# 1 / rms as a power on GpSimd, the router's order written out, and the last tiles' buffers and squares

## The chip, the cores and the metric

The kernel runs on one core of a Trainium2 chip. Its engines each take their instructions in order: PE (TensorE, matrix products and transposes), DVE (VectorE), ACT (ScalarE), Pool (GpSimd) and SP (SyncE, which issues most DMAs). An engine waits on semaphores that the others raise. The metric is the device time of one execution in microseconds (us), here the median of three runs. The profile is of one more execution.

## The reference

Two blocks stand one behind the other, on 512 tokens of width 1024, and then 32 experts take two per token. Cut to what matters here:

```python
def rms_norm(x, g):
    xf = x.astype(jnp.float32)
    xf = xf * lax.rsqrt(jnp.mean(xf * xf, axis=-1, keepdims=True) + RMS_EPS)
    return xf.astype(x.dtype) * g

# first block: even mixer (window attention + retention), cross attention, odd mixer (convolution), cross attention
x = x + even_mixer(rmsnorm(x, e_norm[j]), ...)
x = x + memory_cross_attention(rmsnorm(x, c_norm[i]), rmsnorm(mem, c_mem_norm[i]), ...)
# retention ends each head with
o = o * lax.rsqrt(jnp.mean(o * o, axis=-1, keepdims=True) + EPS)
# second block: three branches, merged, then the router and the experts
x = x + merged @ w_out[l]
h2 = rms_norm(x, ffn_norm_g[l])
g_idx = jnp.argmax(h2 @ w_rg + b_rg); top_p, top_i = lax.top_k(softmax(e_logits of that group), 2)
y[e] = (silu(xb @ w_gate_e[e]) * (xb @ w_up_e[e])) @ w_down_e[e]      # for the tokens sent to expert e
x = x + sum over the token's two experts of weight * y
return rms_norm(x, final_norm_g)
```

## The kernel before

The 512 tokens are held feature-major: a tile of 128 features by 512 tokens for each of eight slices of the width. Almost all products up to 1318 us of the trace are made by `mm3` (L320, L321, L322), three fp32r matmuls for one product, and PE runs them back to back; weights come from HBM as `raw`, and ACT (L249) and DVE (L250) split them in a high and a low part.

**The norms.** For each of them a `Stats` object sums squares in `acc`. `total` (L281) adds them over partitions by four matmuls against ones, `mean` (L288) makes the mean on DVE, `norm_r` calls `rsqrt`, and the broadcast's PE transposes (L295, of a column `r_tok`, `rm_tok`, `n2r` or `rkv_tok`) spread the result over partitions. `rsqrt` (L229 to L244) is nine DVE instructions, most of them on 128x4: two integer steps for a first guess and seven arithmetic ones. It is called 14 times by the retention's four heads (L618), the norms and the router (L1248). Matmuls of other work stand on PE between L281 and L295. A tile scheduler fixes this order when the kernel is built; it is not decided at run time.

**The retention.** For a head, DVE sums squares (L615), makes the mean (L616), runs `rsqrt`, and multiplies the output `oc` by `rr` (L621); PE then transposes `oc` (L628). The state of a head is updated on DVE (L598, `st`), and PE multiplies with it (L607).

**The router.** `e_out(m)` (L1198 on) is called for the eight slices m of the merged output: xk (L1203, DVE), its square (L1205, ACT), four products with the router's weights (L1215, PE), for m = 7 the sums of squares (L1210, PE), four transposes (L1223), the token-major copy xt (L1226, ACT), for m = 7 the scaled copy xg (L1234, Pool) and its split in two parts h (L1236 on ACT, L1237 on Pool), and a store to `hd` in HBM (L1238, SP). Then v5 (L1247), `rsqrt`, the logits L (L1251), a chain of DVE instructions with the group's and the experts' maxima, PE's ranks (L1303), the slots (`slot_keys`, L1311 to L1314, with `key`; `slot_rows`, L1319 to L1331, with `pair`, `lane`, and for each k and t three or four rows `rv`), the count of rounds (`most`, `more`, `nri`), and `moe()`.

**The experts.** `moe()` runs 8 rounds of two pairs of experts. The first round's tokens are gathered by products with one-hot tiles `oh` (L1384, L1385, L1401); later ones by an indirect DMA (L1369) from `hd`. Weights, 96 MiB, come through a ring of 12 buffers `ew`, in 1 MiB transfers that SP issues (L1418, L1426); a transfer waits until PE has done with its buffer. `combine` adds the rounds by products with `comb` (L1483) and adds to `xts` on DVE (L1485, the tile's name in the trace is `merged`).

**The end.** `finish(t)` (L1488) runs for the four tiles of 128 tokens: Pool multiplies the first half with the gain (L1493, `zf`), ACT squares the tile and sums (L1494), DVE makes 1 / rms in seven steps (L1495 to L1504) and the second half of y (L1506), ACT the first half (L1508), and SP stores both (L1507, L1509). The four `zf` come from three buffers.

Of the kernel before, what the change touches and what calls it, by code (L numbers as in the profile page):

```python
# [20 lines left out]
D = 1024  # L21
# [2 lines left out]
EPS = 1e-6  # L24
NE, NL = 4, 8
HEAD0 = 2
FETCH = range(1, 8)
NEG = -1e30


# [133 lines left out]
def body(ctx: ExitStack, tc, A, out):  # L164
# [60 lines left out]
    def V(name, k, n=1):  # L225
        o, _ = VOFF[name]
        return vec[:, o + k:o + k + n]

    def rsqrt(dst, v, n):  # L229

        y = small(n, "rs_y")
        t = small(n, "rs_t", I32)
        b = small(n, "rs_b")
        nc.vector.tensor_scalar(t, v.bitcast(I32), 1, None, op0=ALU.arith_shift_right)
        nc.vector.tensor_scalar(y.bitcast(I32), t, -1, 0x5f3759df, op0=ALU.mult, op1=ALU.add)

        nc.vector.tensor_tensor(b, y, y, op=ALU.mult)
        nc.vector.tensor_tensor(b, v, b, op=ALU.mult)
        nc.vector.scalar_tensor_tensor(b, b, -10.0 / 3, b, op0=ALU.add, op1=ALU.mult)
        nc.vector.scalar_tensor_tensor(y, b, 5.0, y, op0=ALU.add, op1=ALU.mult)  # L240
        c = 0.375
        nc.vector.tensor_tensor(b, y, y, op=ALU.mult)
        nc.vector.scalar_tensor_tensor(b, v, -0.5 * c ** 3, b, op0=ALU.mult, op1=ALU.mult)
        nc.vector.scalar_tensor_tensor(dst, b, 1.5 * c, y, op0=ALU.add, op1=ALU.mult)  # L244

    def split(hi, lo, src, scale=None):

# [951 lines left out]
    def e_out(m, ps):  # L1199
        xk = r_xk()  # L1200
        nc.gpsimd.dma_start(xk, xd[m])
        nc.gpsimd.tensor_tensor(xk, xk, rb1, op=ALU.mult)
        nc.vector.scalar_tensor_tensor(xk, xk, V("final_norm", m), ps, op0=ALU.mult, op1=ALU.add)  # L1203
        sq = acc5 if m == 0 else r_gg()
        nc.scalar.activation(sq, xk, AF.Square)  # L1205
        if 0 < m < 7:
            nc.gpsimd.tensor_tensor(acc5, acc5, sq, op=ALU.add)
        def squares(a, last):
            for t in range(4):
                nc.tensor.matmul(lp[:, 144 + t:145 + t], lhsT=a[:, t * 128:t * 128 + 128], rhs=ones,  # L1210
                                 start=False, stop=last and t == 3)

        for t in range(4):
            c = slice(t * 128, t * 128 + 128)
            nc.tensor.matmul(lg[:, t], lhsT=xk[:, c], rhs=rtw[:, m], start=m == 0 and t == 0, stop=False)  # L1215
        if m == 7:
            squares(sq, True)
        if m == 6:
            squares(acc5, False)
# [97 lines left out]
    def slot_rows(ps):  # L1317

        TT(rtmp2, one2, pair0[:, None, None, :].to_broadcast([128, 2, 4, 32]), op=ALU.mult)  # L1319
        vsum(pair2, rtmp2)  # L1320
        STT(lane2, pair2, -128.0, key2, op0=ALU.mult, op1=ALU.add)
        for k in range(2):
            for t in range(4):
                lh = rp.tile([128, 128], F32, name="lh", tag="lh", bufs=2)
                rv = rp.tile([128, 3, 16], F32, name="rv", bufs=2)
                TS(lh, iota[:, :128], lane[k][:, t:t + 1], None, op0=ALU.is_equal)
                TS(rv[:, 1], iota[:, :16], pair[k][:, t:t + 1], 0.5, op0=ALU.is_equal, op1=ALU.mult)
                TS(rv[:, 0], rv[:, 1], tok[:, t:t + 1], 2.0, op0=ALU.mult, op1=ALU.mult)
                TS(rv[:, 2], rv[:, 1], (w1, w2)[k][:, t:t + 1], 2.0, op0=ALU.mult, op1=ALU.mult)
                TS(rv[:, 1], rv[:, 1], r5[:, t:t + 1], None, op0=ALU.mult)  # L1330
                nc.tensor.matmul(ps, lhsT=lh, rhs=rv.rearrange("p a b -> p (a b)"), start=k == 0 and t == 0,  # L1331
                                 stop=k == 1 and t == 3)
                yield k, t
        nc.vector.tensor_copy(rh, ps[:, 16:32])
        STT(rr, rh, 2.0, rh, op0=ALU.mult, op1=ALU.mult)
        nc.vector.tensor_copy(wt, ps[:, 32:48])
        TS(st, ps[:, :16], -1.0, None, op0=ALU.add)
        TS(st2, st, 0.0, None, op0=ALU.max)
        nc.vector.tensor_copy(sti, st2)
        TS(st2, st, -256.0, None, op0=ALU.add)  # L1340

    slot_keys(pre)
    nc.vector.tensor_copy(rank, pre)

    pn = trps()[:, :32]
    for t in range(4):
# [24 lines left out]

    def gather(j2, between=lambda: None):

        oh, kk, xT = [], [], []
        if j2 not in FETCH:
            for k in range(2):
                x_ = key[k]
                if j2:
                    x_ = hp.tile([128, 4], F32, name="kk", tag="kk", bufs=4)
                    TS(x_, key[k], -256.0 * j2, None, op0=ALU.add)  # L1380
                kk.append(x_)
            for t in range(4):
                x_ = hp.tile([128, 256], F32R, name="oh", tag="oh", bufs=5)
                TS(x_, iota, kk[0][:, t:t + 1], None, op0=ALU.is_equal)  # L1384
                STT(x_, iota, kk[1][:, t:t + 1], x_.bitcast(F32), op0=ALU.is_equal, op1=ALU.add)  # L1385
                oh.append(x_)
        for f2_ in range(4):
            if f2_ % 2 == 0:
                xs = xy.tile([128, D], F32, name="xT", tag="xT", bufs=3).rearrange("p (a i s) -> p a i s", a=2, i=2)
            ps = pq.tile([128, 2, 256], F32, name="pg", tag="pg", bufs=2)  # L1390
            for i in range(2):
                f = 2 * f2_ + i
                if j2 in FETCH:
                    for k in range(2):
                        nc.tensor.transpose(ps[:, i, k * 128:k * 128 + 128], fetched[j2][k][:, f * 128:f * 128 + 128],  # L1395
                                            ident)
                    continue
                for t in range(4):
                    c = slice(t * 128, t * 128 + 128)
                    for part in range(2):  # L1400
                        nc.tensor.matmul(ps[:, i], lhsT=h2[f][part][:, c], rhs=oh[t],  # L1401
                                         start=t == 0 and part == 0, stop=t == 3 and part == 1)
            between()
            x_ = xs[:, f2_ % 2]
# [83 lines left out]
    def finish(t, fg, y):  # L1488

        H = D // 2  # L1490
        ss = small(1, "fss")
        zf = xy.tile([128, D], F32, name="zf", tag="xT", bufs=3)
        nc.gpsimd.tensor_tensor(zf[:, :H], xts[t][:, :H], fg[:, :H], op=ALU.mult)  # L1493
        nc.scalar.activation(y, xts[t], AF.Square, accum_out=ss)  # L1494
        TS(ss, ss, 0.5 / D, 0.5 * EPS, op0=ALU.mult, op1=ALU.add)  # L1495
        rf, b, i = small(1, "frr"), small(1, "rs_b"), small(1, "rs_t", I32)
        TS(i, ss.bitcast(I32), 1, None, op0=ALU.arith_shift_right)  # L1497
        TS(rf.bitcast(I32), i, -1, 0x5f3759df - (1 << 22) - (1 << 31), op0=ALU.mult, op1=ALU.add)

        STT(b, rf, ss, rf, op0=ALU.mult, op1=ALU.mult)  # L1500
        STT(b, b, -5.0 / 3, b, op0=ALU.add, op1=ALU.mult)  # L1501
        STT(rf, b, 1.25, rf, op0=ALU.add, op1=ALU.mult)  # L1502
        STT(b, rf, ss, rf, op0=ALU.mult, op1=ALU.mult)  # L1503
        STT(rf, b, -2.0 / 3, rf, op0=ALU.add, op1=ALU.mult)  # L1504
# [6 lines left out]
    def moe():  # L1511
# [11 lines left out]
        last = []  # L1523
        for i in range(8):
            a, b, more_ = 2 * i, 2 * i + 1, i < 7
            if i + 1 in FETCH:
                fetched[i + 1] = fetch(i + 1)
            pa = gu(a, xT, wga)
            if more_:
# [26 lines left out]
        nc.vector.tensor_scalar(fg, fg, 3.375, None, op0=ALU.mult)  # L1556
        for t in combine(last):
            finish(t, fg, ew()[:, :D])

# [35 lines left out]
```

## Time and profile before

| | us |
|---|---|
| median of 3 runs (range) | 1618.24 (1617.14 to 1618.45) |
| the profiled execution | 1614.45 |
| its span, first to last instruction | 1612.7 |
| PE busy | 1557.1 (97%) |
| DVE busy | 915.5 (57%) |
| ACT busy | 604.8 (38%) |
| Pool busy | 115.5 (7%) |
| PE waiting for another engine or a DMA, all together | 36.8 |

The span is what the page of the profile covers; about 1.75 us of the execution lie around it. The mean granted TensorE clock is 0.991 of full speed. The page cuts the span in 40 slices of 40.3 us; slices 33 to 39 are the router, the experts and the end.

### The profile page before, as it was taken

The numbers are of one execution on the slowest core, as the hardware profiler recorded it, in microseconds if no ns is written. First come the engines' busy times: TensorE is split into PE (matmuls) and PEld (weight loads), VectorE is DVE, ScalarE is ACT, GpSimd is POOL, SyncE is SP. The second block draws the span as 40 slices with busy tenths as digits, with TensorE's granted clock in tenths as the row PEclk, the third lists the DMA queues.
The fourth block names the chain that finished last, engine by engine and source line by source line (L and its number), as shares of the span: only waits on it lengthen the run. The fifth ranks groups of instructions, "written<-read, shape, count | busy, mean of one in ns | idle before, by whom it ended". The sixth has DMA issues, their size and how long they took to land. (4 is left out here: it accounts for less than half of the span.)

```text
span 1612.7 us, 20331 instructions
## 1 busy us (share of the span) xinstructions
PE 1557.1 (97%) x7958; PEld 1206.7 (75%) x7958; DVE 915.5 (57%) x1697; ACT 604.8 (38%) x1060; POOL 115.5 (7%) x104
## 2 busy tenths in 40 slices
PE   7999999999999999999999999999999978999996
PEld 6758898888888889888887777888888865454443
DVE  5577675456555565555776776485544555343335
ACT  5455244344323244434545554244433421111212
POOL 0000200000011110000100000000111340000001
PEclk9999999999999999999999999999999989999998
DMA  6312244221222235320411112333422439999993
GB/s 213 105 53 79 79 134 154 82 76 53 105 81 103 104 131 183 105 105 26 165 54 55 54 55 80 110 137 114 165 105 93 142 93 369 419 421 420 420 420 138
DMA packets 44375, 241.91 MB, mean 150 GB/s; under 512 B 6112, under 2 KB 11104, under 8 KB 18160
## 3 DMA queue, kind: packets, MB, share of 16 engines
q1 hardware_dynamic: 40944, 228.93, 37.9%
q0 software_dynamic: 3328, 11.60, 2.0%
q8 instruction: 65, 1.06, 0.3%
q14 instruction: 38, 0.31, 0.1%
HBM read 234.22 MB, written 6.29 MB: 149 GB/s over the span
## 5 line engine op out<-in xcount | busy, mean ns | idle before, releaser
L249 ACT ACTIVATE w<-raw 128x1024 fp32r<-128x1024 f32 (+2 forms) x242 | 234.1, 968 | 413.7 <-PE mm L322 377.4
L320 PE MATMUL mm<-xg,w 128*128 128x512 f32 x864 | 341.3, 395 | 8.6 <-ACT xg L252 7.9
L321 PE MATMUL mm<-xg,w 128*128 128x512 f32 x864 | 341.3, 395 | 0.0
L322 PE MATMUL mm<-xg,w 128*128 128x512 f32 x864 | 340.3, 394 | 0.8 <-DVE w L250 0.8
L250 DVE TENSOR_TENSOR w<-raw,w 128x1024 fp32r<-128x1024 f32 (+2 forms) x242 | 280.0, 1159 | 105.6 <-ACT w L249 104.3
L320 PEld LDWEIGHTS mm<-xg,w 128*128 128x128 f32 x864 | 163.4, 189 | 42.2 <-ACT xg L252 7.9
L322 PEld LDWEIGHTS mm<-xg,w 128*128 128x128 f32 x864 | 163.1, 189 | 34.4 <-DVE w L250 1.2
L321 PEld LDWEIGHTS mm<-xg,w 128*128 128x128 f32 x864 | 163.1, 189 | 34.1 <-issue 2.0
L321 PE MATMUL mm<-y,w 128*128 128x512 f32 x448 | 174.9, 390 | 0.0
L322 PE MATMUL mm<-y,w 128*128 128x512 f32 x448 | 174.9, 391 | 0.0
L320 PE MATMUL mm<-y,w 128*128 128x512 f32 x448 | 174.3, 391 | 0.0
L1436 PE MATMUL pgu<-ew,xT 128*64 128x512 f32 x512 | 112.8, 594 | 0.0
L320 PEld LDWEIGHTS mm<-y,w 128*128 128x128 f32 x448 | 83.9, 188 | 17.7 <-ACT y L249 1.2
L321 PEld LDWEIGHTS mm<-y,w 128*128 128x128 f32 x448 | 84.2, 188 | 17.2 <-DVE y L250 0.4
L322 PEld LDWEIGHTS mm<-y,w 128*128 128x128 f32 x448 | 84.2, 188 | 17.2
L1436 PEld LDWEIGHTS pgu<-ew,xT 128*64 128x64 f32 x512 | 36.1, 137 | 71.0 <-issue 71.0
L1483 PE MATMUL py<-ys,comb 128*128 128x512 f32 x256 | 62.3, 397 | 0.0
L1443 DVE SCALAR_TENSOR_TENSOR eth<-eth,pgu 128x256 f32<-128x256 f32 x16 | 6.7, 422 | 95.1 <-ACT eth L1442 95.1
L1462 PE MATMUL py<-ew,aT 128*64 128x512 f32 x256 | 58.1, 596 | 1.2 <-ACT aT L1452 1.2
L1483 PEld LDWEIGHTS py<-ys,comb 128*128 128x128 f32 x256 | 46.9, 188 | 15.9 <-issue 5.7
L1442 ACT ACTIVATE eth<-pgu,rh 128x256 f32<-128x256 f32 x16 | 7.6, 474 | 130.8 <-PE pgu L1436 130.8
L389 DVE TENSOR_TENSOR x<-mm,x 128x512 f32<-128x512 f32 x32 | 22.1, 692 | 50.1 <-PE mm L322 50.1
(446 smaller groups left out, 2475.9 us busy)
## 6 DMA issues: line engine op xcount, KB each, us to landing
ew<-in_egu_dram SPq DMA_DIRECT2D x64, 1024.0 KB, 17.5
ew<-in_edn_dram SPq DMA_DIRECT2D x32, 1024.0 KB, 18.5
raw<-in_wkv_dram SPq DMA_DIRECT2D x20, 1024.0 KB, 4.7
raw<-in_ow_dram SPq DMA_DIRECT2D x16, 1024.0 KB, 4.7
raw<-in_ew_dram SPq DMA_DIRECT2D x12, 1024.0 KB, 4.8
raw<-in_w2gate_dram SPq DMA_DIRECT2D x12, 1024.0 KB, 4.8
raw<-in_wq_dram SPq DMA_DIRECT2D x8, 1024.0 KB, 4.8
raw<-in_wo_dram SPq DMA_DIRECT2D x8, 1024.0 KB, 4.7
```

The lines of the kernel that those rows point to most:

```text
L249: nc.scalar.activation(hi, src, AF.Copy)
L250: nc.vector.tensor_tensor(lo, src, hi.bitcast(F32), op=ALU.subtract)
L320: nc.tensor.matmul(ps, lhsT=lh, rhs=rh, start=first, stop=False)
L321: nc.tensor.matmul(ps, lhsT=lh, rhs=rl, start=False, stop=False)
L322: nc.tensor.matmul(ps, lhsT=ll, rhs=rh, start=False, stop=last)
L389: nc.vector.tensor_tensor(x[:, m], ps, x[:, m], op=ALU.add)
L1436: nc.tensor.matmul(ps[64 * i:64 * i + 64], lhsT=xT[k][:, o + 64 * i:o + 64 * i + 64], rhs=W[2 * (k // 4) + i][:, k % 4], start=k == 0, sto ...
L1442: nc.scalar.activation(th, pg_[:, :256], AF.Tanh, scale=rh[:, j:j + 1])
L1443: STT(th, th, 1.0, pg_[:, :256], op0=ALU.add, op1=ALU.mult)
L1462: nc.tensor.matmul(py[64 * i:64 * i + 64], lhsT=aT[:, f, 64 * i:64 * i + 64], rhs=W[i][:, f, n * 512:n * 512 + 512], start=f == 0, stop=f ...
L1483: nc.tensor.matmul(py, lhsT=comb[:, t * 128:t * 128 + 128], rhs=y[:, c], start=i == 0, stop=i == len(parts) - 1)
```

## The change

Three parts. First, `rsqrt` becomes one Pool instruction, v to the power of -0.5, against a constant tile `nhalf` (128x8); `finish` calls it too, with the gain scaled by 32 and the sum of squares plus D * EPS. Second, the router: for m = 7, xk and its square are made in two halves of 256 columns, and the transposes, xt, xg, h and the store of m = 7 (now `flipped(7)`) stand behind the power on Pool, in an order written out; `slot_rows` makes each `rv` by three instructions that don't hang on each other, with r5h = 0.5 * r5; the one-hots are four tiles of their own (`oh0`), made on DVE right behind `slot_keys`, in an order written out, ahead of the copy `rank`. Third, the end: tile 3's `zf` has a buffer of its own, and its squares are made in two halves.

```diff
+    nhalf = cp.tile([128, 8], F32, name="nhalf")
+    nc.vector.memset(nhalf, -0.5)
+
     def rsqrt(dst, v, n):
 
-        y = small(n, "rs_y")
-        t = small(n, "rs_t", I32)
-        b = small(n, "rs_b")
...
-        nc.vector.scalar_tensor_tensor(dst, b, 1.5 * c, y, op0=ALU.add, op1=ALU.mult)
+        nc.gpsimd.tensor_tensor(dst, v, nhalf[:, :n], op=ALU.pow)
...
-        nc.vector.scalar_tensor_tensor(xk, xk, V("final_norm", m), ps, op0=ALU.mult, op1=ALU.add)
         sq = acc5 if m == 0 else r_gg()
-        nc.scalar.activation(sq, xk, AF.Square)
+        for h in range(1 if m < 7 else 2):
+            c = slice(0, 512) if m < 7 else slice(h * 256, h * 256 + 256)
+            nc.vector.scalar_tensor_tensor(xk[:, c], xk[:, c], V("final_norm", m), ps[:, c], op0=ALU.mult, op1=ALU.add)
+            nc.scalar.activation(sq[:, c], xk[:, c], AF.Square)
...
     rsqrt(r5, v5, 4)
+
+    r5h = rtile("r5h", 4)
+    with tc.manual_schedule(engines={mybir.EngineType.Pool}):
+        nc.gpsimd.tensor_scalar(r5h, r5, 0.5, None, op0=ALU.mult)
+        flipped(7, late[0])
...
-                TS(rv[:, 1], iota[:, :16], pair[k][:, t:t + 1], 0.5, op0=ALU.is_equal, op1=ALU.mult)
-                TS(rv[:, 0], rv[:, 1], tok[:, t:t + 1], 2.0, op0=ALU.mult, op1=ALU.mult)
-                TS(rv[:, 2], rv[:, 1], (w1, w2)[k][:, t:t + 1], 2.0, op0=ALU.mult, op1=ALU.mult)
-                TS(rv[:, 1], rv[:, 1], r5[:, t:t + 1], None, op0=ALU.mult)
+                for a, v in enumerate((tok, r5h, (w1, w2)[k])):
+                    TS(rv[:, a], iota[:, :16], pair[k][:, t:t + 1], v[:, t:t + 1], op0=ALU.is_equal, op1=ALU.mult)
...
-    slot_keys(pre)
-    nc.vector.tensor_copy(rank, pre)
+    with tc.manual_schedule(engines={mybir.EngineType.DVE}):
+        slot_keys(pre)
+        one_hots()
+        nc.vector.tensor_copy(rank, pre)
...
-        zf = xy.tile([128, D], F32, name="zf", tag="xT", bufs=3)
+        zf = xy.tile([128, D], F32, name="zf", tag="xT" if t < 3 else "xg", bufs=3 if t < 3 else 2)
...
+        if t < 3:
+            nc.scalar.activation(y, xts[t], AF.Square, accum_out=ss[:, :1])
+            TS(ss[:, :1], ss[:, :1], D * EPS, None, op0=ALU.add)
+        else:
+            for h in range(2):
+                c = slice(h * H, h * H + H)
+                nc.scalar.activation(y[:, c], xts[t][:, c], AF.Square, accum_out=ss[:, h:h + 1])
+            STT(ss[:, :1], ss[:, :1], D * EPS, ss[:, 1:], op0=ALU.add, op1=ALU.add)
+        rsqrt(rf, ss[:, :1], 1)
```

With the nine instructions gone the scheduler also orders anew. On PE at the kernel's first norm, before (L320 to L322 are the products of the even mixer's input):

```order
L281 MATMUL tr<-ones,acc 128x1 x4
L320 MATMUL mm<-xg,w 128x512
L321 MATMUL mm<-xg,w 128x512
L322 MATMUL mm<-xg,w 128x512
...
L321 MATMUL mm<-xg,w 128x512
L322 MATMUL mm<-xg,w 128x512
L295 MATMUL tr<-ident,r_tok 128x128 x4
```

and now (the lines of the file have moved by 11, so L309 to L311 are the products, L284 the transposes):

```order
L270 MATMUL tr<-ones,acc 128x1 x4
L309 MATMUL mm<-xg,w 128x512
L310 MATMUL mm<-xg,w 128x512
L284 MATMUL tr<-ident,r_tok 128x128 x4
L311 MATMUL mm<-xg,w 128x512
```

Nine matmuls stood between the sums and the transposes that need r, and now two. It is the same at the other norms: 13 and now 2 at the odd mixer's, 16 and now 2 at `rkv_tok`, 9 and now 3 at `n2r`, 16 and now 1 at the first `rm_tok`, 12 and now 6 at the second.

On DVE in the retention, at the second head's sums, before (`st` is the state that PE's L607 waits for):

```order
L616 TENSOR_SCALAR ss<-ss 128x4
L234 TENSOR_SCALAR rs_t<-ss 128x4
...
L239 SCALAR_TENSOR_TENSOR rs_b<-rs_b 128x4
L598 SCALAR_TENSOR_TENSOR st<-st,sc 128x128
L240 SCALAR_TENSOR_TENSOR rs_y<-rs_b,rs_y 128x4
L598 SCALAR_TENSOR_TENSOR st<-st,sc 128x128
...
L244 SCALAR_TENSOR_TENSOR rr<-rs_b,rs_y 128x4
L621 TENSOR_SCALAR oc<-oc,rr 128x128 x4
```

and now:

```order
L605 TENSOR_SCALAR ss<-ss 128x4
L610 TENSOR_SCALAR oc<-oc,rr 128x128 x4
L587 SCALAR_TENSOR_TENSOR st<-st,sc 128x128 x2
L599 SCALAR_TENSOR_TENSOR oc<-tr,qdec,oc 128x384
L619 SCALAR_TENSOR_TENSOR gate<-tr,gate 128x512
```

The state's update stood inside the chain of nine, and now stands behind `oc`, which waits for Pool's `rr`. Two of the four heads have this form.

On Pool, at the end of the router (L1234 and L1237 are xg and h of m = 7 and keep their numbers; `misc` is the sum of squares of the slices before) and at the end of the kernel, now:

```order
L1198 TENSOR_TENSOR misc<-misc,gg 128x512
L233 TENSOR_TENSOR r_10586<-v_10585,nhalf 128x4
L1252 TENSOR_SCALAR r5h<-r_10586 128x4
L1234 TENSOR_TENSOR xg<-merged,gb 128x512
L1237 TENSOR_TENSOR h_10599<-xg,h_10599 128x512
...
L1494 TENSOR_TENSOR zf<-merged,ew 128x512 x2
L233 TENSOR_TENSOR frr<-fss,nhalf 128x1
L1494 TENSOR_TENSOR zf<-merged,ew 128x512
L233 TENSOR_TENSOR frr<-fss,nhalf 128x1
L1494 TENSOR_TENSOR zf<-merged,ew 128x512
L233 TENSOR_TENSOR frr<-fss,nhalf 128x1 x2
```

Before, xg and h followed `misc` at once, and the four `zf` stood in a row with nothing between. On DVE at the end, each tile's second half of y now stands ahead of the next tile's sum, and on ACT the first two tiles' y ahead of the third tile's squares, where before all four squares stood ahead of the four y.

## Rows read from the trace of the kernel before

**Rows 1.** The head of the page: the span, and the busy time of the engines with its share and the instructions.

```profile
span 1612.7 us, 20331 instructions
...
PE 1557.1 (97%) x7958; PEld 1206.7 (75%) x7958; DVE 915.5 (57%) x1697; ACT 604.8 (38%) x1060; POOL 115.5 (7%) x104
```

**Rows 2.** The waits of PE over the whole span, by the line that waits and by what ended the wait: total us, times, longest.

```profile
PE tr L1303 <- DVE hot L1299: 8.7, 1, 8.7
...
PE pg L1401 <- DVE oh L1385: 3.0, 1, 3.0
PE po L1215 <- DVE xk L1203: 2.6, 2, 1.3
...
PE tr L628 <- DVE oc L621: 1.4, 1, 1.4
...
PE tr L295 <- DVE rm_tok L244: 0.4, 1, 0.4
...
PE tr L295 <- DVE n2r L244: 0.2, 1, 0.2
```

**Rows 3.** The timeline at the first norm, 24 to 36 us: start, duration, engine and line; in brackets the idle time before and what ended it.

```profile
24.89 0.16 DVE L288 TENSOR_SCALAR mean<-tr 128x4 f32<-128x4 f32 x1 [1.23 <-PE tr L281]
...
25.27 0.40 PE L322 MATMUL mm<-xg,w 128*128 128x512 f32 x1
...
26.68 0.16 DVE L244 SCALAR_TENSOR_TENSOR r_tok<-rs_b,rs_y 128x4 f32<-128x4 f32 x1
...
26.89 0.65 PE L295 MATMUL tr<-ident,r_tok 128*128 128x128 f32 x4
```

**Rows 4.** Groups of instructions of Pool, different shapes apart: count, busy us in all, mean ns of one, idle before.

```profile
L1493 POOL TENSOR_TENSOR zf<-merged,ew 128x512 f32<-128x512 f32 x4 | 5.2, 1301 | 69.1 <-DVE merged L1485 65.1 <-ACT ew L1508 3.5 <-DVE frr L1498 0.5
...
L1079 POOL MEMSET pu<- 128x48 f32 x4 | 0.5, 137 | 88.7 <-DVE pool L1091 58.5 <-PE po L322 30.2
...
L1583 POOL MEMSET const-float32-1.0<- 128x1 f32 x1 | 0.1, 102 | 0.0
```

**Rows 5.** The timeline of the retention's second head, 151 to 161 us.

```profile
155.91 0.17 DVE L616 TENSOR_SCALAR ss<-ss 128x4 f32<-128x4 f32 x1
...
157.05 0.29 DVE L598 SCALAR_TENSOR_TENSOR st<-st,sc 128x128 f32<-128x128 f32 x1
...
157.43 0.83 PE L607 MATMUL tr<-st,rot 128*128 128x128 f32 x6
...
158.16 0.88 DVE L621 TENSOR_SCALAR oc<-oc,rr 128x128 f32<-128x128 f32 x4
```

**Rows 6.** The timeline of the router, 1311 to 1362 us.

```profile
1319.29 0.63 ACT L1205 ACTIVATE gg<-xk 128x512 f32<-128x512 f32 x1 [5.03 <-DVE xk L1203]
...
1321.88 0.16 DVE L1247 TENSOR_SCALAR v<-po 128x4 f32<-128x4 f32 x1 [2.63 <-PE po L1210]
...
1322.87 1.26 POOL L1234 TENSOR_TENSOR xg<-merged,gb 128x512 f32<-128x512 f32 x1 [10.16 <-DVE rs_b L238]
1322.88 1.27 DVE L239 SCALAR_TENSOR_TENSOR rs_b<-rs_b 128x4 f32<-128x4 f32 x1
1324.16 0.63 ACT L1236 ACTIVATE h<-xg 128x512 fp32r<-128x512 f32 x1 [1.37 <-POOL xg L1234]
...
1324.87 1.26 POOL L1237 TENSOR_TENSOR h<-xg,h 128x512 fp32r<-128x512 f32 x1 [0.74 <-ACT h L1236]
1324.96 0.74 DVE L1251 SCALAR_TENSOR_TENSOR L<-po,r,bb 128x36 f32<-128x36 f32 x4
...
1326.83 0.28 DVE L1280 TENSOR_TENSOR lane_e<-L,go 128x128 f32<-128x128 f32 x1
...
1331.73 0.28 DVE L1343 COPY rank<-tr 128x128 f32<-128x128 f32 x1
...
1335.08 0.88 DVE L1385 SCALAR_TENSOR_TENSOR oh<-iota,key,oh 128x256 fp32r<-128x256 bf16 x2
1335.87 0.42 DVE L1319 TENSOR_TENSOR rtmp<-one,c_pair 128x256 f32<-128x256 f32 x1
```

**Rows 7.** The timeline near the end, 1588 to 1613 us.

```profile
1594.15 1.30 POOL L1493 TENSOR_TENSOR zf<-merged,ew 128x512 f32<-128x512 f32 x1 [0.29 <-DVE merged L1485]
...
1594.83 0.14 DVE L1495 TENSOR_SCALAR fss<-fss 128x1 f32<-128x1 f32 x1
...
1595.13 0.69 DVE L1485 TENSOR_TENSOR merged<-py,merged 128x512 f32<-128x512 f32 x1
...
1595.96 1.34 POOL L1493 TENSOR_TENSOR zf<-merged,ew 128x512 f32<-128x512 f32 x1 [0.51 <-DVE frr L1498]
...
1596.65 0.67 DVE L1501 SCALAR_TENSOR_TENSOR rs_b<-rs_b 128x1 f32<-128x1 f32 x1
...
1598.94 1.06 ACT L1494 ACTIVATE ew<-merged 128x1024 f32<-128x1024 f32 x1 [1.02 <-DVE merged L1485]
...
1604.37 0.72 ACT L1508 ACTIVATE ew<-zf,frr 128x512 f32<-128x512 f32 x1 [0.61 <-DVE frr L1504]
```

**Rows 8.** The timeline, SP's issue of the last two expert weights (1 MiB each) and PE's first matmuls with the last of them.

```profile
1560.51 0.84 SPq L1426 DMA_DIRECT2D ew<-in_edn_dram  x2
...
1586.62 3.65 PE L1462 MATMUL py<-ew,aT 128*64 128x512 f32 x16 [0.72 <-ACT aT L1452]
```

**Rows 9.** The DMA issues of 1559 to 1563 us: count, KB each, median us from issue to landing.

```profile
ew<-in_edn_dram SPq DMA_DIRECT2D x2, 1024.0 KB, 18.7
```

More of the change, by code (lines that the diff above doesn't have):

```diff
@@ L26 @@
 HEAD0 = 2
-FETCH = range(1, 8)
 NEG = -1e30
@@ L227, in V @@
         return vec[:, o + k:o + k + n]
+    nhalf = cp.tile([128, 8], F32, name="nhalf")
+    nc.vector.memset(nhalf, -0.5)
     def rsqrt(dst, v, n):
-        y = small(n, "rs_y")
-        t = small(n, "rs_t", I32)
-        b = small(n, "rs_b")
[L234 to L243, printed above, removed]
-        nc.vector.scalar_tensor_tensor(dst, b, 1.5 * c, y, op0=ALU.add, op1=ALU.mult)
+        nc.gpsimd.tensor_tensor(dst, v, nhalf[:, :n], op=ALU.pow)
     def split(hi, lo, src, scale=None):
@@ L1217, in e_out, with flipped @@
             squares(sq, True)
-        if m == 6:
-            squares(acc5, False)
+            late.append(xk)
+        else:
+            if m == 6:
+                squares(acc5, False)
+            flipped(m, xk)
+    late = []
+    def flipped(m, xk):
         pt = trps()
@@ L1340, in slot_rows, with one_hots @@
         TS(st2, st, -256.0, None, op0=ALU.add)
-    slot_keys(pre)
-    nc.vector.tensor_copy(rank, pre)
+    oh0 = [rtile(f"oh{t}", 256, dt=F32R) for t in range(4)]
+    def one_hots():
+        for t, o in enumerate(oh0):
+            TS(o, iota, key[0][:, t:t + 1], None, op0=ALU.is_equal)
+            STT(o, iota, key[1][:, t:t + 1], o.bitcast(F32), op0=ALU.is_equal, op1=ALU.add)
+    with tc.manual_schedule(engines={mybir.EngineType.DVE}):
+        slot_keys(pre)
+        one_hots()
+        nc.vector.tensor_copy(rank, pre)
     pn = trps()[:, :32]
@@ L1372, in gather @@
     def gather(j2, between=lambda: None):
[L1374 to L1386, printed above, removed]
+        xT = []
         for f2_ in range(4):
@@ L1392, in gather @@
                 f = 2 * f2_ + i
-                if j2 in FETCH:
+                if j2:
                     for k in range(2):
@@ L1400, in gather @@
                     for part in range(2):
-                        nc.tensor.matmul(ps[:, i], lhsT=h2[f][part][:, c], rhs=oh[t],
+                        nc.tensor.matmul(ps[:, i], lhsT=h2[f][part][:, c], rhs=oh0[t],
                                          start=t == 0 and part == 0, stop=t == 3 and part == 1)
@@ L1490, in finish @@
         H = D // 2
-        ss = small(1, "fss")
-        zf = xy.tile([128, D], F32, name="zf", tag="xT", bufs=3)
+        ss, rf = small(2, "fss"), small(1, "frr")
+        zf = xy.tile([128, D], F32, name="zf", tag="xT" if t < 3 else "xg", bufs=3 if t < 3 else 2)
         nc.gpsimd.tensor_tensor(zf[:, :H], xts[t][:, :H], fg[:, :H], op=ALU.mult)
[L1494 to L1504, printed above, removed]
+        if t < 3:
+            nc.scalar.activation(y, xts[t], AF.Square, accum_out=ss[:, :1])
+            TS(ss[:, :1], ss[:, :1], D * EPS, None, op0=ALU.add)
+        else:
+            for h in range(2):
[3 more added lines that the diff above has]
+        rsqrt(rf, ss[:, :1], 1)
         o = out[0, t * 128:t * 128 + 128]
@@ L1525, in moe @@
             a, b, more_ = 2 * i, 2 * i + 1, i < 7
-            if i + 1 in FETCH:
+            if more_:
                 fetched[i + 1] = fetch(i + 1)
@@ L1555, in moe @@
         nc.sync.dma_start(fg, A["fing"].to_broadcast([128, D]))
-        nc.vector.tensor_scalar(fg, fg, 3.375, None, op0=ALU.mult)
+        nc.vector.tensor_scalar(fg, fg, 32.0, None, op0=ALU.mult)
         for t in combine(last):
@@ L1569, in body @@
         slot_keys(rtmp)
+        one_hots()
         with tc.manual_schedule(engines={mybir.EngineType.PE}):
```

## The prediction

> **What bounds the kernel now.** First the head of the page [rows 1]: PE is busy for 1557.1 of 1612.7 us, no other engine for more than 57%. So an edit counts only where PE waits for it, or where PE has nothing left to do. Next the waits of PE [rows 2], which add to 36.8 us. The reader is to see that the greatest, 8.7 us, is the router's chain on DVE (PE's ranks wait for `hot`), with 3.0 us for the first one-hots and 2.6 us for the last xk; the retention's `oc` costs 1.4 us once, and the norms' columns only 0.4 and 0.2 us. Then the timelines of the first norm [rows 3], the retention [rows 5], the router [rows 6] and the end [rows 7], for who follows whom. Last, whether the experts' weights would swallow what the router gains [rows 8, 9]: the last two transfers are issued at 1560.51 and land 18.7 us later, so at 1579.2 or, counted from the issue's end, 1580.1; PE first uses them at 1586.62. That leaves some 6.5 us of slack, and PE is the bound of the rounds. A round's transfers wait for PE to free buffers, so an earlier start of PE starts them earlier too. A microsecond gained ahead of the experts therefore reaches the end.
>
> **The unknown price d.** Everything hangs on how long one power takes on Pool; no row shows one. Pool's nearest rows [rows 4]: a memset of 128x1 takes 0.10 us and one of 128x48 0.14 us, which bounds d from below; a product of 128x512 takes 1.30 us, which bounds it from above for 1 to 8 columns, unless the power costs more than some hundred times a product for each element. That a power beats 0.10 us is excluded by the memset, which computes nothing. The shape (128x4, 128x1) is near the memsets, the function dearer than a product. I take d = 0.3 us, an estimate near the low end, and keep 0.10 and 1.26 for the range. A handover between engines is about 0.1 us each way: xg ends on Pool at 1324.13 and ACT begins at 1324.16; h ends on ACT at 1324.79 and Pool begins at 1324.87 [rows 6].
>
> **Part 1: the norms.** The nine instructions took from 24.89 + 0.16 to 26.68 + 0.16, so 1.8 us [rows 3], and nine matmuls lay beside them: PE waited for nothing there. Now two lie there. The mean ends at 25.05; the power runs from about 25.15 to 25.15 + d; PE has done with its two matmuls when the third of before begins, 25.27 [rows 3]. The transposes can go at about 25.25 + d, so PE idles for about d. Five norms have one to three matmuls of cover and cost d each (the one with six has more than they need and is counted at nothing). What goes is the wait of before, 0.4 + 0.2 us [rows 2]; `n2r` keeps its 0.2, since its transposes stood late already with nine matmuls of cover. Term: **0.4 - 5d**. The matmuls that stood there stand behind now, the same ones: no work is saved or added on PE.
>
> **Part 2: the retention.** The wait of 1.4 us for `oc` [rows 2] goes: with one instruction in place of nine, `oc` is early. But two heads have `st` behind `oc`. Before, the second head's mean ended at 156.08 and `st`'s first update at 157.34, and PE began with it at 157.43 [rows 5]. Now: power from 156.2 to 156.2 + d, `oc` takes 0.88, `st` 0.29, so `st` at 157.45 + d: 0.1 + d later, twice, and PE is waiting there. Term: 1.4 - 2(0.1 + d) = **1.2 - 2d**.
>
> **Part 3: the router.** From the mean (1321.88) to `lane_e` (1326.83) are 4.95 us before [rows 6]. In place of the nine: the mean 0.16, two handovers 0.2, d, the logits 0.74, and from their end (1325.70) to `lane_e` 1.13 as before, together 2.23 + d. Against that, two products of Pool, xg and h, move from beside `rsqrt` to beside the chain of maxima. One such meeting is in the trace: while Pool's xg runs (1322.87, 1.26 us), the DVE instruction that begins at 1322.88 takes 1.27 us, the mean beside it in the chain 0.16 [rows 6]; the logits, which read PSUM, run at 1324.96 beside Pool's h and aren't held. Now xg begins right behind r5h, beside the logits, and holds the first of the maxima's two-input steps for about 0.46 us; the Exp stands behind the copy h on ACT (0.38); h's 1.26 us hold a third step for 0.94. Sum 1.8, so 4.05 + d, and the chain gains 0.9 - d.
>
> The Trainium skill, SBUF — State Buffer, section "Who interferes with whom", speaks against this part of the change: VectorE and GpSimd share one port pair under an exclusive lock, and whoever comes second blocks for the other's whole instruction. The trace agrees (0.16 against 1.27 us); by that rule the router gains 0.9 - d, and without such a lock it would gain 2.7 - d.
>
> The rest of the router: halves of xk and of its square let the square of the first half (0.32 of 0.63) run beside the second half of xk, but PE's order with two columns of tokens at a time keeps only about 0.15 of it. The copy `rank` (0.28, begun at 1331.73) leaves the way of `key`; half of it lay beside other work: 0.1. One-hots now alternate with `pair` (0.42), `lane` and the first `rv`, so that the last of them ends about 1 us later relative to `key` (before, all lay in a row to 1335.96 and the product for `pair` began at 1335.87 [rows 6]); PE needs that only for the second half of its first group, 0.25 us lost. The lighter rows `rv` save DVE eight instructions of 0.23, beside PE's products, so nothing. The moved steps of m = 7 feed the gather and a store to `hd` that is ahead of eight weight transfers on SP's queue; they come up to 0.4 us later and are used at 1334.38 at the earliest, so hidden. Term: **0.9 - d**.
>
> **Part 4: the end.** Before, the fourth square begins at 1598.94, and the last y ends at 1604.37 + 0.72 = 1605.09 [rows 7]: four chains of seven are mixed on DVE. With the power the first sum is done at about 1595.0, `zf` of tile 1 ends on Pool at 1595.45, and the first power ends at 1595.5 + d, about when the add for tile 2 ends (1595.82). From there it goes in series, since ACT has the first two y ahead of the third square and Pool has `zf` between the powers: `zf` of tile 2 to 1597.2; y of tile 0 on DVE held until then (as at 1596.65, 0.67 in place of 0.16 beside a Pool product [rows 7]), to 1597.95; the sum, the power of tile 1 to 1598.2 + d; its y on ACT to 1599.0 + d; the square of tile 2 to 1600.3 + d; `zf` of tile 3 on Pool meanwhile, to 1601.6; the power of tile 2 to 1601.7 + d; y of tile 2, 0.72, and the second half of the last square, 0.8 with its sum, to 1603.25 + d; sum, power, and the last y to 1604.3 + 2d. Term: 1605.1 - 1604.3 - 2d = **0.8 - 2d**. At the end, then, four squares ahead of all y are given up for a chain of powers, and the gain of the shorter chain is spent again.
>
> **The sum.** (0.4 - 5d) + (1.2 - 2d) + (0.9 - d) + (0.8 - 2d) = 3.3 - 10d. At d = 0.3 that is 0.3 us gained: 1614.45 becomes 1614.15 by the profiled execution. That one lies 3.8 us under the median of the runs; I carry the difference over, 1618.24 - 0.3 = **1617.9**. At d = 0.10 the gain is 2.3, at 0.65 there are 3.2 us lost, at 1.26 there are 9.3. Break-even is d = 0.33. A measurement of this kernel tells 0.2%, 3.2 us, from no change. For d of 0.15 to 0.55 the forecast's own range is 1616.4 to 1620.4, and with 1.5 us for the terms' sizes 1615 to 1622.
>
> **Rivals.**
> - **The power is longer than its cover (slower).** One mechanism: DVE hands to Pool and PE, in order, stands behind. It decides at the PE transposes of the norms, where two matmuls lie and nine lay, and is slower beyond measurement from d = 0.65. For it: Pool's product of 128x512 takes 1.30 us, and a power is more than a product [rows 4]. Against: 4 columns are few. At d = 0.8 it gives -4.7, 1623; at 1.26, 1627.5. Chance 0.26.
> - **Pool holds DVE less than I count, and the power is short (faster).** If the products fall between DVE's two-input steps rather than on them, the router gets back its 1.8 us and the end up to 1.3, and with d = 0.10 that is 2.3 + 3.1 = 5.4: 1613. For it: the logits weren't held [rows 6]. Against: both meetings in the trace cost the rest of Pool's instruction [rows 6, 7]. Chance 0.14.
> - **The new order of the body.** The scheduler moved whole stretches of PE's products. The waits of PE outside the router, the retention and the end add to about 12 of the 36.8 us, mostly at the start of products that wait for ACT or DVE; the order could take back or add a third of it, 4 us. Gain 1614, loss 1622. Chance 0.12 for the gain and 0.04 for the loss.
>
> **How the numbers follow.** The forecast has 0.44. Faster by over 0.2%: 0.14 + 0.12 and 0.01 at the edge of the forecast's own range, 0.27. Slower: 0.26 + 0.04 and 0.02 at the other edge, 0.32. The same: the rest of the forecast, 0.41. The range of 1613 to 1625 leaves out half of the second rival (0.07) below, and above the part of the first with d over 1.0 (0.09).
>
> **What would show it.** On Pool, the rows of the power: mean under 0.35 us for break-even. In the waits of PE, new ones for `r_tok`, `rkv_tok`, `n2r` and `rm_tok` of about d each, and none for `oc` of 1.4. In the router, `lane_e` 4.3 us after the mean, with two-input DVE steps of over 0.9 us beside Pool's h. At the end, the last y 0.2 us closer to the last combining product. I am wrong if the power is far from 0.3 us, if the transposes don't wait, or if the body's products shift by more than 2 us.

## The result and the profile after

The changed kernel takes 1630.24 us (median of 4 runs, 1629.99 to 1630.86) where before, timed beside it, takes 1618.35 us. By these medians it is 11.9 us slower, 0.73%; the ratio on record is 1.0081, with a 95% interval of [1.0069, 1.0094]. The forecast was 1617.9, with a range up to 1625.

The profiled execution of the changed kernel takes 1630.86 us, 16.4 more than that of before. This is more than the medians differ, and the clock shows why: executions of before aren't alike. Of 23 timed in one later session, those with a mean granted clock of 0.991 took 1614.7 to 1615.1 us and those with 0.987 took 1620.0 to 1621.4; the profiled one of before had 0.991. The changed kernel had 0.985 or 0.986 in all four. From the page after, to be held against [rows 1]; the line PEclk is the granted clock in tenths, in 40 slices:

```profile
span 1629.0 us, 20197 instructions
...
PE 1565.1 (96%) x7958; PEld 1213.0 (74%) x7958; DVE 894.4 (55%) x1537; ACT 604.7 (37%) x1063; POOL 135.0 (8%) x123
...
PEclk9999999999999999999999999999999998999998
```

PE is busy for 8 us more with the same 7958 instructions, so some of them ran slower. The price of a power, which nothing in the trace of before showed, is in the groups of Pool:

```profile
L233 POOL TENSOR_TENSOR r_tok<-mean,nhalf 128x4 f32<-128x4 f32 x4 | 5.1, 1286 | 255.7 <-DVE mean L277 255.7
...
L233 POOL TENSOR_TENSOR rr<-ss,nhalf 128x4 f32<-128x4 f32 x4 | 4.0, 1012 | 54.2 <-DVE ss L605 54.2
L233 POOL TENSOR_TENSOR frr<-fss,nhalf 128x1 f32<-128x1 f32 x4 | 2.2, 558 | 2.3 <-DVE fss L1502 1.6 <-DVE fss L1497 0.7
...
L233 POOL TENSOR_TENSOR n2r<-n2v,nhalf 128x8 f32<-128x8 f32 x1 | 1.6, 1650 | 5.1 <-DVE n2v L825 5.1
L233 POOL TENSOR_TENSOR rm_tok<-mean,nhalf 128x2 f32<-128x2 f32 x2 | 1.4, 706 | 145.5 <-DVE mean L277 145.5
```

0.56 us for one column, 0.71 for two, 1.01 for four, 1.65 for eight: about 0.40 us and 0.155 for each column. The waits of PE, which answer to [rows 2] (total, times, longest):

```profile
PE tr L1308 <- DVE hot L1304: 9.0, 1, 9.0
...
PE pg L1402 <- DVE rank L1356: 5.9, 1, 5.9
PE tr L701 <- ACT aP L694: 4.5, 3, 1.6
...
PE tr L284 <- POOL r_tok L233: 2.7, 2, 1.9
...
PE tr L284 <- POOL n2r L233: 1.4, 1, 1.4
...
PE tr L596 <- DVE st L587: 1.0, 2, 0.5
PE tr L617 <- DVE oc L610: 1.0, 1, 1.0
PE tr L284 <- POOL rkv_tok L233: 0.9, 1, 0.9
...
PE tr L284 <- POOL rm_tok L233: 0.5, 1, 0.5
```

Five waits for norms stand where two stood, 5.5 us in place of 0.6; `st` is new; `aP`, the first attention's softmax, has 4.5 where before had

```profile
PE tr L712 <- ACT aP L705: 1.5, 2, 1.1
```

and the first gather product waits 5.9 us, for the copy `rank` this time, where it waited 3.0 for the one-hots.

What a wait for r_tok does beyond its length is in the timeline of the odd mixer's norm, the counterpart of [rows 3]:

```profile
430.75 0.16 DVE L277 TENSOR_SCALAR mean<-tr 128x4 f32<-128x4 f32 x1 [2.64 <-PE tr L270]
...
431.06 1.23 DVE L239 TENSOR_TENSOR w<-raw,w 128x1024 fp32r<-128x1024 f32 x1
431.06 2.09 POOL L233 TENSOR_TENSOR r_tok<-mean,nhalf 128x4 f32<-128x4 f32 x1 [99.17 <-DVE mean L277]
...
433.20 0.65 PE L284 MATMUL tr<-ident,r_tok 128*128 128x128 f32 x4 [1.91 <-POOL r_tok L233]
```

and in 2 us windows (PE busy, and third from the end the granted clock):

```profile
432.00:434.00 2.00, 0.80 (x6) 0.76 (x7) 0.28 (x1) 0.11 (x1) 1.15 (x1) 1.00 0.29 53
434.00:436.00 2.00, 2.00 (x7) 1.54 (x6) 1.38 (x2) 0.49 (x1) 0.00 (x0) 0.62 0.91 381
436.00:438.00 2.00, 2.00 (x6) 1.60 (x5) 0.00 (x0) 0.00 (x0) 0.00 (x0) 0.53 0.25 98
438.00:440.00 2.00, 2.00 (x10) 1.66 (x9) 0.00 (x0) 0.00 (x0) 0.00 (x0) 1.00 0.00 0
```

The weight split on DVE and the power begin together; the power takes 2.09 us in place of 1.0. PE idles for 1.91 us, and then its clock is at the lower level for 3.4 us, with 6 products in a window where 10 belong (they begin 0.43 us apart, at 435.16 and 435.58, and 0.23 apart behind the stretch, at 438.25 and 438.48). Six such stretches lie ahead of the router: at 100 and 117 (behind waits for aP of 1.64 and 1.48 us), 434, 820 (behind n2r), 1093 and 1298 us. The profiled execution of before has none.

The router, the counterpart of [rows 6], and the end, of [rows 7]:

```profile
1336.58 0.16 DVE L1247 TENSOR_SCALAR v<-po 128x4 f32<-128x4 f32 x1 [1.99 <-PE po L1202]
1336.82 1.02 POOL L233 TENSOR_TENSOR r<-v,nhalf 128x4 f32<-128x4 f32 x1 [8.51 <-DVE v L1247]
...
1338.86 0.59 DVE L1269 TENSOR_TENSOR go<-L,gm 128x16 f32<-128x16 f32 x1
...
1340.29 1.15 DVE L1272 TENSOR_TENSOR go<-go,gb 128x16 f32<-128x16 f32 x1
...
1341.47 0.29 DVE L1285 TENSOR_TENSOR lane_e<-L,go 128x128 f32<-128x128 f32 x1
...
1351.51 0.28 DVE L1356 COPY rank<-tr 128x128 f32<-128x128 f32 x1
...
1351.94 3.76 PE L1402 MATMUL pg<-oh,h 128*128 128x256 f32 x16 [5.90 <-DVE rank L1356]
```

```profile
1612.74 1.30 POOL L1494 TENSOR_TENSOR zf<-merged,ew 128x512 f32<-128x512 f32 x1
1612.78 1.81 DVE L1505 SCALAR_TENSOR_TENSOR ew<-merged,frr,ew 128x512 f32<-128x512 f32 x1 [0.18 <-POOL frr L233]
...
1620.76 0.72 ACT L1507 ACTIVATE ew<-zf,frr 128x512 f32<-128x512 f32 x1 [0.86 <-POOL frr L233]
```

From the mean to `lane_e` it is 4.89 us, before 4.95. Two-input steps on DVE are held by xg (0.59) and h (1.15), the end's first y by `zf` (1.81), as forecast.

Five marks in the traces divide the 16.4 us: the start of PE's ranks, the first gather product, the first expert product, the first product of the last combine, and the end of the last y. Before they are at 1330.86, 1334.38, 1346.61, 1590.20 and 1605.09 us, after at 1345.51, 1351.94, 1363.37, 1606.95 and 1621.48:

| stretch | before | after | lost |
|---|---|---|---|
| start to ranks | 1330.86 | 1345.51 | 14.65 |
| ranks to gather | 3.52 | 6.43 | 2.91 |
| gather to experts | 12.23 | 11.43 | -0.80 |
| experts to last combine | 243.59 | 243.58 | 0.0 |
| last combine to last y | 14.89 | 14.53 | -0.36 |

Up to the ranks PE is idle for 40.0 us (1345.51 less 1305.5 busy) where it was idle for 33.6 (1330.86 less 1297.3). The other 8.2 of the 14.65 are longer busy time; put down to the six stretches at the lower clock, that is 1.4 us for each.

### The profile page after: what moved, and what is told of

Read it like the earlier page. It is cut to its first block, busy times and chain, and to the rows that moved or that the text cites. A ratio compares the mean times of both kernels' runs of the same rounds, so it can differ in the third digit from the quotient of the medians.

```text
span 1629.0 us, 20197 instructions
## 1 busy us (share of the span) xinstructions
PE 1565.1 (96%) x7958; PEld 1213.0 (74%) x7958; DVE 894.4 (55%) x1537; ACT 604.7 (37%) x1063; POOL 135.0 (8%) x123
## 5 line engine op out<-in xcount | busy, mean ns | idle before, releaser
L309 PE MATMUL mm<-xg,w 128*128 128x512 f32 x864 | 343.0, 397 | 8.3 <-ACT xg L241 8.3
L311 PE MATMUL mm<-xg,w 128*128 128x512 f32 x864 | 342.0, 396 | 0.0
L309 PEld LDWEIGHTS mm<-xg,w 128*128 128x128 f32 x864 | 164.5, 190 | 41.9 <-ACT xg L241 8.3
L311 PEld LDWEIGHTS mm<-xg,w 128*128 128x128 f32 x864 | 164.1, 190 | 32.9 <-issue 0.3
L311 PE MATMUL mm<-y,w 128*128 128x512 f32 x448 | 175.2, 392 | 0.0
L309 PE MATMUL mm<-y,w 128*128 128x512 f32 x448 | 174.4, 392 | 0.0
L309 PEld LDWEIGHTS mm<-y,w 128*128 128x128 f32 x448 | 84.1, 189 | 18.0 <-ACT y L238 1.2
L311 PEld LDWEIGHTS mm<-y,w 128*128 128x128 f32 x448 | 84.4, 188 | 17.1
L1486 DVE TENSOR_TENSOR merged<-py,merged 128x512 f32<-128x512 f32 x64 | 44.1, 690 | 10.6 <-PE py L1484 9.3
## 6 DMA issues: line engine op xcount, KB each, us to landing
ew<-in_egu_dram SPq DMA_DIRECT2D x64, 1024.0 KB, 16.4
```

What stands on the lines that cost most here:

```text
L309: nc.tensor.matmul(ps, lhsT=lh, rhs=rh, start=first, stop=False)
L311: nc.tensor.matmul(ps, lhsT=ll, rhs=rh, start=False, stop=last)
L1486: TT(xts[t][:, c], py, xts[t][:, c], op=ALU.add)
```

## The experiments

Theory 1: the power is three times as dear as I took it, PE stands idle behind it, and a longer gap costs again through the clock. Rivals: the loss sits in the router and the end; or it comes from the new order of the body, whatever a power costs. Within a session all share the runs of before, whose median is 1616.4 (runs 1 to 4), 1617.34 (5 to 8) and 1617.47 (9 and 10).

**1, the power in the body alone.** Before, with:

```diff
+    def powr(dst, v, n):
+
+        nc.gpsimd.tensor_tensor(dst, v, nhalf[:, :n], op=ALU.pow)
...
-        rsqrt(r, v, nt)
+        powr(r, v, nt)
```

The last two lines are those of the norms; it is the same at the memory norms, the retention and `n2r`.

> The kernel before, with the power on GpSimd in the norms and the retention alone; the router and the end keep the nine and seven DVE instructions and their old order. Theory 1 (the power is dear, 1.0 us for 4 columns by the trace of the changed kernel, PE idles behind it, and where a gap of PE is over some 1.3 us the granted clock then halves for 3.4 us, which costs 1.7 us): the body carries nearly all of the loss, 10 to 11 us, so 1628 to 1630, with half-clock stretches behind the transposes of r_tok and n2r. Theory 2 (the loss sits in the router and the end): 1618 to 1620.

Measured 1626.16, ratio 1.0063 [1.0048, 1.0078], 10 us slower than before in its session. PE's ranks start at 1339.77, 8.9 later than before. The waits are those of the changed kernel: r_tok 2.7, aP 4.5, n2r 1.4, rkv_tok 0.9. Stretches at the lower clock are fewer in this execution, three ahead of the router (114, 432 and 817 us).

**2, the nine instructions back in the body.** The changed kernel, with the power at r5 and in `finish` only.

> The changed kernel, with the nine DVE instructions back in the norms and the retention; the router and the end as changed, with the power. Theory 1: the body is as before, the router costs 2 us (PE's first gather product waits for the copy rank, which now stands behind all one-hots on DVE) and the end gains 0.4, so about 1620. Theory 2: 1627 or more.

Measured 1616.22, ratio 1.0000 [0.9989, 1.0010]. The body carries the loss; router and end together cost nothing that can be measured. I had expected 1.6 us there. Its trace has the same 5.9 us wait for `rank` and loses 1.8 between the ranks and the experts, and gains 0.7 ahead of the ranks and 0.4 at the end.

**3, one cheap instruction in place of the power.**

```diff
-        nc.gpsimd.tensor_tensor(dst, v, nhalf[:, :n], op=ALU.pow)
+        nc.vector.reciprocal(dst, v)
```

> The changed kernel with one DVE reciprocal in place of each power, so that 1/v stands where 1/sqrt(v) belongs: the price of about 1.0 us and the two handovers go, the order on PE stays nearly that of the changed kernel. Theory 1: the waits of PE for r_tok, n2r, rkv_tok and rm_tok (5.5 us together) and the two half-clock stretches behind them (3.4 us) go, and some 2 us of the router and the end: 1619 to 1621. Rival (the new order of the first attention and of the body costs the time, whatever the power's price): 1626 or more, with the waits for aP of 4.5 us and the half-clock stretches at 100 and 117 us still there and most of the loss.

With 1/v the values are other ones, further rounds run (112 indirect gathers in place of 14), and the whole takes 3576.85 us; only the part up to the ranks can be compared, which start at 1330.5, 15 us ahead of the changed kernel and 0.4 ahead of before. The reciprocal takes 0.18 us for 128x4. The order on PE is nearly that of the changed kernel: one matmul of cover more at r_tok and rkv_tok (three in place of two) and at n2r (four in place of three), and at the first rm_tok four small ones more. The waits for r_tok, n2r, rkv_tok and rm_tok and the stretches at 434 and 820 us are gone. But the rival holds a share of it: the wait for aP stays. The timeline, and a window behind it:

```profile
93.80 2.30 POOL L550 TENSOR_TENSOR rot<-rot,rotb 128x512 f32<-128x512 f32 x1 [14.30 <-DVE rotb L549]
...
94.89 1.23 DVE L689 TENSOR_TENSOR asum<-asum,aes 128x8 f32<-128x8 f32 x1
...
97.02 0.72 PE L701 MATMUL tr<-ident,aP 128*128 128x128 f32 x2 [1.64 <-ACT aP L694]
```

```profile
98.00:100.00 2.00, 2.00 (x9) 1.81 (x8) 1.57 (x5) 0.76 (x2) 0.00 (x0) 0.50 0.00 0
```

In the new order a product of Pool lies under the softmax's sum on DVE, which takes 1.23 us for 128x8, and aP is late; there is nothing else for PE to do, and the clock falls. That belongs to the order, which the power and the reciprocal both bring. What it costs over the whole body can be read at the start of the last product ahead of the router: 1317.65 before, 1319.10 here, 1333.23 in the changed kernel. So this order with the cheap instruction is 1.5 us later than before, the waits for aP and their stretches counted in, and the power in its place takes the other 14.1; the lead of 0.4 us at the ranks comes from the router.

**4, the copy `rank` ahead of the one-hots.**

```diff
         slot_keys(pre)
-        one_hots()
         nc.vector.tensor_copy(rank, pre)
+        one_hots()
```

> The changed kernel with the copy rank ahead of the one-hots on DVE, no other change of order. If PE's first gather product waits for that copy (5.9 us in the trace of the changed kernel against 3.0 before): 2 us less, 1628. If the one-hots themselves are what it waits for: no change, 1630.

Measured 1628.39, ratio 1.0071 [1.0055, 1.0086]. The wait for the gather is 3.1 us again:

```profile
1346.42 0.28 DVE L1355 COPY rank<-tr 128x128 f32<-128x128 f32 x1
...
1347.90 5.18 PE L1402 MATMUL pg<-oh,h 128*128 128x256 f32 x16 [3.06 <-DVE oh L1351]
```

So PE did wait for that copy, by 2.8 us (6.43 to 3.60 from the ranks). But from the gather to the experts it now takes 13.11 in place of 11.43, since PE comes earlier and is still at the lower clock: 1.2 us are left of it.

**5, both.** The second kernel with the fourth's copy.

> The kernel of the second run (nine DVE instructions in the norms and the retention, the router and the end as changed, with the power) with the copy rank ahead of the one-hots. If the router's new order loses only by that copy: 2 us less than the second run, so 1614 where before is 1616.4, faster than both kernels. If the fourth run's gain was chance: 1616.

Measured 1615.54, ratio 0.9991 [0.9982, 1.0000]. Hardly told from before, and in the trace nothing came of the earlier gather: 14.02 us to the experts, of which the first groups run at the lower clock up to 1342 us.

**6, nine instructions at two norms.** The fourth kernel, with r_tok and rm_tok of the even mixer on DVE.

> The kernel of the fourth run (changed, rank first) with nine DVE instructions in two of the norms alone, the even mixer's (r_tok) and the first memory norm (rm_tok); the retention and all later norms keep the power. With these two the order on PE in the first attention is that of before again. If that order costs what the trace shows: the waits for aP fall from 4.5 to 1.5 us, the half-clock stretches at 98 and 116 us go (3.4 us), and 0.8 us of the wait for r_tok: 7 us less than the fourth run, about 1621. If only the power's own waits count: 1 us less, 1627.

Measured 1622.50, ratio 1.0032 [1.0019, 1.0045]. That is 5.2 us above before in its session, where the fourth run was 12.0 above: 7 us less, as expected. The wait for aP is back at 1.5, and the stretches at 98 and 116 us are gone. Not all agrees: r_tok of the odd mixer still has its gap of 1.91 us, and in this execution no stretch behind it, while the one behind n2r lasts 7 us.

```profile
PE tr L305 <- POOL r_tok L238: 1.9, 1, 1.9
...
PE tr L722 <- ACT aP L715: 1.5, 2, 1.1
```

**7, no power.** The router's new order and `rank` first, nine instructions throughout, the end as before.

> No power at all: nine DVE instructions everywhere, the end as before; the router's new order, with its halves and lighter rows, and rank first. Against the fifth run this shows what the power is worth in the router and at the end. By the sum with d = 1.0 and 0.56 in place of 1.8 and of seven steps: 1 us worse than the fifth run, 1615. If the power at these two places is worth nothing: the same as the fifth.

Measured 1616.22, ratio 0.9998 [0.9989, 1.0007], and the fifth kernel has 0.9991: the intervals don't separate them. The trace has PE's wait for `hot` at 9.6 us against 9.0, and the end at 14.92 against 14.50, so the power is worth 0.6 and 0.4 us in these two places.

**8, work for PE while the power runs.** The fourth kernel with:

```diff
         ps = trps()
+        for _ in range(10):
+            nc.tensor.transpose(ps[:, :128], ident, ident)
         for t in range(nt):
             nc.tensor.transpose(ps[:, t * 128:t * 128 + 128], r[:, t:t + 1].to_broadcast([128, 128]), ident)
```

> The kernel of the fourth run with ten throwaway transposes (1.6 us) on PE ahead of the transposes of each norm's broadcast, so that PE works while the power runs; their result is written over. If it is PE's gap that brings the half clock: no stretch behind r_tok at 434 us and n2r at 820 us, 3.4 us less there, against up to 0.5 us for each of seven norms where the throwaway work stands ahead of real products: 1624 to 1628, with a clock of 0.987 or more. If the half clock comes by itself: the stretches stay and it is 1629 to 1631.

```profile
433.65 1.29 PE L284 MATMUL tr<-ident 128*128 128x128 f32 x10
...
436.28 0.65 PE L286 MATMUL tr<-ident,r_tok 128*128 128x128 f32 x4 [1.34 <-POOL r_tok L233]
```

```profile
436.00:438.00 2.00, 1.72 (x10) 1.50 (x11) 0.40 (x1) 0.60 (x1) 0.23 (x1) 1.00 0.78 213
438.00:440.00 2.00, 2.00 (x10) 1.63 (x9) 0.98 (x2) 0.00 (x0) 0.00 (x0) 1.00 0.74 311
```

With 1.29 us of work there is no stretch behind r_tok, nor behind n2r; those of the first attention (one of them some 7 us long) and one at 1096 us remain. Still it takes 1629.81, ratio 1.0076 [1.0062, 1.0090]. That is above the 1624 to 1628 expected if PE's gap brings the half clock, and within the 1629 to 1631 of the rival, so the time doesn't decide between them; only the trace speaks for the gap. The throwaway work is itself the likely reason, though no run separates it: ten transposes at each of seven broadcasts are 9.0 us, and PE is busy for 1572.9 us where the fourth kernel has 1566.0. Two of six executions had a clock of 0.991 and 0.992 and took 1627.4 and 1626.7. What the power's waits cost without the stretches can't be read from this run.

**9 and 10, work for PE in the router.** 76 transposes of `ident` ahead of the ranks and 24 ahead of the gather, in the fifth kernel and in before:

```diff
+    fl = trps()[:, :128]
+    for _ in range(76):
+        nc.tensor.transpose(fl, ident, ident)
     pre = trps()[:, :128].rearrange("p (t e) -> p t e", t=4)
```

> The kernel of the fifth run with throwaway transposes on PE where it waits for the router: 76 (about 8 us) ahead of the ranks, 24 (2.5 us) ahead of the first gather; nothing reads their result. In all traces so far PE is at half clock from about 1 us into the router's wait, and stays there for 4 to 8 us of the gather. If PE's idleness is what brings the half clock and working in the wait prevents it: the gather takes 10 to 11 us in place of 14.0, and the kernel 3 us less than the fifth run's 1615.5, about 1612.5. If throwaway work doesn't hold the clock: 1615 to 1617.

> The kernel before with the same throwaway transposes at the same two places. If the half clock comes from PE's idleness: its gather takes 10.5 us in place of 12.2, 1.5 us less than before's median. If not: the same as before, or up to 1 us more where the throwaway work stands ahead of the ranks.

```profile
1320.77 8.38 PE L1325 MATMUL tr<-ident 128*128 128x128 f32 x75
1329.93 0.18 PE L1329 MATMUL tr<-hot,before 128*128 128x32 bf16 x1 [0.78 <-DVE hot L1322]
...
1333.91 0.99 PE L1426 MATMUL pg<-oh,h 128*128 128x256 f32 x4
...
1345.06 5.37 PE L1461 MATMUL pgu<-ew,xT 128*64 128x512 f32 x24
```

The ninth takes 1614.05, ratio 0.9979 [0.9969, 0.9988], faster than both kernels, though 1.5 us less than the fifth where 3 were expected. The gather takes 11.15 us in place of 14.02, and no window ahead of the end is below the full clock. The tenth, before with the same, takes 1615.90, ratio 0.9991 [0.9981, 1.0001]; its gather takes 11.38 in place of 12.23. All twelve executions of each show the higher mean clock: 0.994 to 0.997 and 0.993 to 0.996, against 0.987 to 0.991 of before in that session. Idle PE brings the lower clock, and throwaway work prevents it: that is shown here at the router in two kernels. Run 8's one trace points the same way at n2r; at r_tok it can't tell, since run 6's trace has no stretch there either, without any throwaway work.

## Why the prediction was wrong

**The price d.** The step that failed first is "I take d = 0.3 us, an estimate near the low end". Measured: 0.56 for one column, 1.01 for four, 1.65 for eight, and 2.09 for four beside a split on DVE. The bound of 1.26 holds the first two and not the others. The text placed the value by the shape (few columns, so near a memset) and hardly by the function, which is what it should have gone by. The first rival, "longer than its cover", names the mechanism and the place; it had 0.26.

**The terms, at the measured price.** The norms' 0.4 - 5d gives -4.6 at d = 1.0, and PE's waits went from 0.6 to 5.5: -4.9. The retention's 1.2 - 2d gives -0.8, and `st` with `oc` waits 2.0 in place of 1.4: -0.6. The end's 0.8 - 2d gives -0.3 at 0.56, and it gained 0.36. Their sizes are off by the price and at most 0.7 us more. In the router 0.9 - d gives -0.1 from the mean to the ranks, and it is +0.05 (8.98 to 8.93). In the norms and the router the mechanism was right. In the retention the sum agrees by luck: `oc`, whose wait was to go, still has 1.0 us of it, and `st` waits 0.5 twice where 0.1 + d, now 1.1, was added for each.

**The sum at that price is still 6 us short**, -5.8 against -11.9 by the medians. Three steps are missing or have the wrong sign.
- "PE idles for about d": an idle PE was counted at its own length. It also brings a stretch at the lower clock, which at 1.4 us each makes 8.2 of the profiled execution's 16.4. Not all of these belong to the change: the two at 1093 and 1298 us lie behind gaps that before has too (0.76 and 0.65 us at the one place in both; 1.33 at the other, now 1.51), and before's own executions differ by 5 us with the clock.
- The order of the body was left as a rival of 4 us with more chance for gain. In the first attention it cost 3.0 us of waits and two stretches, as runs 3 and 6 show from both sides. By run 3 most of this comes back elsewhere in the body as long as the instruction is cheap, 1.5 us are left; what loses is this order together with a dear one.
- "The copy `rank` leaves the way of `key`: 0.1" has the wrong sign. PE's first gather product waits for the copy, and 2.9 us were lost between ranks and gather. Less of it counts in the end: 0.8 came back ahead of the experts, and with the copy moved run 4 gained 1.2 us up to there and run 5 nothing. That no wait in before's trace named the copy was no evidence that nobody waits for it: there it was early.

**What held.** Pool's products hold DVE's two-input steps beside them (0.59 and 1.15 in the router, 1.81 at the end), the rule of the Trainium skill, SBUF — State Buffer, section "Who interferes with whom", that was weighed there. Only I read it one way. It also holds the power itself: 2.09 us beside a DVE split of 1.23, against 1.01. A short Pool instruction beside a DVE that splits weights has that price too. The halves of the last xk gave about what was forecast, 0.2 us in place of 0.15: from the start of the last product to the mean it is 3.35 us (1333.23 to 1336.58), and 3.56 in run 1 (1327.38 to 1330.94), which has the old router and the full clock there. Before has 4.23 (1317.65 to 1321.88), but its xk began 0.85 us behind the product's start, in place of 0.49 in the other two, and its clock fell at 1321.0 us, which cost it another 0.3; with the full clock, in run 10, it is 3.92. That part of the profiled difference is luck. And the experts absorb nothing: 243.58 against 243.59 us.

**Open.** Not every gap of 1.9 us was followed by a stretch (run 6), and gaps of 1.33 and 1.4 us in before's profiled execution were not [rows 2]. Over all twelve traces, ahead of the router, 11 of 14 gaps of 1.48 to 1.95 us were followed by one, and 6 of 18 gaps of 1.31 to 1.43. The length alone doesn't decide: the gap of 1.37 us at `n2r` was followed by a stretch in all four traces that have it, the one of 1.37 us at the retention's `oc` in none of six. The limit of some 1.3 us in run 1's expectation isn't borne out, and what decides stays open. The runs don't add up to the whole either: run 1 is 9.8 us above before and run 2 at 0.2 below, against 11.9 for the change; the changed kernel's trace has six stretches and run 1's three, and why is open too. How much of the 8.9 us of run 1 a power would cost in the old order on PE wasn't tried.

## What to carry to other kernels

An instruction that a trace doesn't show should be priced by its function first and its size second; fewer instructions can be the longer chain. When a scheduler writes the order, one instruction in place of nine can lose the cover that the nine had, here one to three matmuls at five norms in place of nine to sixteen: look in the order for how many matmuls still stand between producer and consumer, and count the new gaps, with what the clock does behind them. Where PE must wait for several microseconds ahead of a PE-bound stage, work that nobody reads can be worth its place.

## What the runs showed of the hardware

- A power on GpSimd takes 0.56, 0.71, 1.01 and 1.65 us for 1, 2, 4 and 8 columns of 128 partitions, and 2.09 in place of 1.01 where it meets a two-input DVE instruction of 1.23 us.
- Of 14 gaps of PE of 1.48 to 1.95 us in an otherwise busy stretch 11 were followed by the lower clock, in the changed kernel for about 3.4 us and at a cost of some 1.4 us each; behind the router's 9 us of idleness the lower clock lasted for another 3.2 (run 1) to 9.5 us (run 6) of work. In runs 9 and 10, 128x128 transposes of a constant were enough to hold the clock there.
